# Column sums in column tiles of four, modulation rows moved from pw1 to pw2, and column reductions behind all rows

## The chip, the cores and the metric

The program runs on one core of one Trainium2 chip. The metric is the time that the device takes for one execution, in microseconds (us). Inside a core the engines are named as the profile names them: TensorE (PE for its matmuls, PEld for its weight loads), VectorE (DVE), ScalarE (ACT), GpSimd (POOL) and SyncE (SP), whose queue issues the loads from HBM. Each engine works through its own instructions in the order in which the program holds them; engines wait for each other on semaphores.

## What is computed

The program is a decoder trunk of two layers for one sequence: D = 2048 channels, T = 256 positions, all float32. Layer 0 mixes tokens with a convolution module, layer 1 with attention; a ConvFFN follows each. Only layer 0's mixer and the entry of its FFN bear on the change:

```python
def ada_ln(c, w, b):
    mod = jax.nn.silu(c) @ w + b
    shift, scale, gate = jnp.split(mod, 3, axis=-1)
    return shift[:, None, :], scale[:, None, :], gate[:, None, :]

def conformer_conv_module(h, pw1_w, pw1_b, dw_w, dw_b, ln_g, ln_b, pw2_w, pw2_b):
    u = h @ pw1_w + pw1_b
    val, gt = jnp.split(u, 2, axis=-1)
    u = val * jax.nn.sigmoid(gt)
    u = causal_depthwise_conv(u, dw_w, dw_b)              # width 31
    u = jax.nn.silu(layer_norm(u, ln_g, ln_b))
    return u @ pw2_w + pw2_b
...
    shift, scale, gate = ada_ln(c, mix_mod_w[i], mix_mod_b[i])
    h = rms_norm(x, mix_norm_g[i]) * (1.0 + scale) + shift
    x = x + gate * y                                      # y: the mixer's result for h
    shift, scale, gate = ada_ln(c, ffn_mod_w[i], ffn_mod_b[i])
    h = rms_norm(x, ffn_norm_g[i]) * (1.0 + scale) + shift
    x = x + gate * conv_ffn(h, ...)
```

## The kernel before

**Layout.** Channels lie on the 128 partitions in KD = 16 tiles of 128 channels, positions on the free axis (256 columns). x, the convolution's output ys[0..15] and its products live in SBUF as 128x256 tiles. TensorE's accumulators (PSUM) are eight banks of 512 columns; the names ps, auxa and auxb in the profile are those banks.

**Weights.** Each product streams its weights in "pieces" of eight 128x128 blocks (512 KB, tile `raw`). pw1 multiplies the float32 piece as it is (`pw1_piece`, L612, matmuls at L620). All later products take three passes of a rounded type: `split_next` (L222) makes a high part wh on ScalarE (L230) and a low part wl on VectorE (L234), and `gemm` (L257) issues high x high, high x low and low x high (L283 to L285). SyncE's queue holds all loads in program order (`load`, L211).

**Modulations.** c is one vector, so each modulation vector (2048 values) is a matrix-vector product. The kernel has two ways for it. *Columns*: a tile of 128 outputs by 2048 inputs (1 MB, tile `mraw`) is multiplied and summed on VectorE (`mod_reduce`, L311). *Rows*: a chunk of four 128x512 blocks of the matrix as it lies (1 MB) goes through TensorE (`mod_rows`, L524): four matmuls at L537, each in its own quarter of 32 columns of the array (`tile_position`), add to one bank, auxa; when the rows of a group are complete, ScalarE copies them and TensorE turns them into columns (L552). `load_rows` (L508) loads the chunks ahead; their buffers are a ring of 3 `mraw` and 4 `mrow` tiles (MORE_ROWS). The groups (`rows_of`, L502) are the mixer's gate (16 chunks), the FFN's scale (16 chunks) and the first `rows0` = ROWS = 2 x 512 values of the FFN's shift (8 chunks); the remaining eight tiles of that shift go through VectorE as columns. `mods0` (L566) is the generator of all this: each `advance(fill, 1)` takes one more step. Before pw2 its steps are row chunks; once `nrow["bias"]` is set (L808), two of three steps also issue one column tile (load and reduction).

**The convolution stage** (L697 to L768) is a loop written out by hand: channel tile c = 0 to 16, in each s = 0 to 18. At each s VectorE gets one of the 19 of 31 taps that it computes (`conv_tap`, L643; taps of channels c and c - 1 alternate), ScalarE the products of the other 11 (`conv_prod`, L652), which GpSimd adds up (L737). At s = 0, 7 and 14 TensorE gets pieces of pw1; at the steps of ROWS_AT (L34) a row chunk: one each at s = 11 of c = 1 to 6, 8, 9, 10 and 12, five each in c = 14 and 15, two in c = 16, and ROWS_TAIL = 4 behind the loop. ScalarE's sigmoid and VectorE's product (`gate_act` L625, `gate_mul` L629) make the convolution's input u of channel j from pw1's accumulators.

**The layer norm's sums.** They run over channels, so over partitions: a matmul with `ones_d` (128x128, each 1/2048) adds a tile's partitions into a bank of 256 columns. `y_sum` (L664) does that at s = 3 for channel c - 2: y0 to y7 in one bank, y8 to y15 in another. From the first bank `first_mean` (L670) takes a first mean m1 at c = 11, which is subtracted from every tile (`y_centre`) before it is squared (`y_square`, ScalarE) and its square summed (`y_square_sum`, L683, at the end of each c). Behind the loop dm, var and the reciprocal root follow (L776 to L785), then for each channel z = silu(...) and its two parts (L797, L799, L357, L358), which pw2 multiplies.

**pw2** (L821): 32 pieces; after each, `tick` advances the modulations by RATES["pw2"], 0.65 steps. Its eight first blocks run side by side (`halves=8`). For each finished block, `pw2_done` (L814) scales on ScalarE, adds to x on VectorE (L817) and makes the parts of x for the FFN (`Entry.add`, L418; L424, L425). `need` (L339) drains modulations that are still missing when a consumer asks. Then the FFN's first product (up00a) begins; it needs the reciprocal root of x's mean square (L391) and two columns with the shift (`scaled`, L457, tile bcol).

**Order.** From L722 to the end of the stage, `in_order` (L191) keeps the four compute engines' instructions as the code issues them; elsewhere a scheduler decides, with the gemm's `done` at high priority.

## Time and profile before

| What | us |
|---|---|
| median of 3 runs (2336.69 to 2341.48) | 2337.83 |
| the profiled execution's own time | 2339.05 |
| its span in the profile | 2336.9 |
| TensorE busy (matmuls), in 17812 instructions | 2278.6 (98%) |
| VectorE busy | 1740.2 (74%) |
| ScalarE busy | 1162.2 (50%) |
| GpSimd busy | 263.6 (11%) |

The profile is of one execution; times in it are from the start of its span. In a row of the timeline stand the start, the duration, the engine, the line, the operation, the tiles (written <- read), their shape, how many instructions the row joins, and in brackets how long the engine was idle before it and what ended that. Rows of the chain of waits give start, duration, engine, tile and line of the work that the end of the program hangs on. A row of the windows gives for a stretch its length, the busy time of PE, PEld, DVE, ACT and POOL with the number of instructions, then the granted TensorE clock, the share of the DMA engines and GB/s. A matmul's duration in a row is from its entry to its end; matmuls overlap, so the step from one start to the next is what one costs.

### The profile page before, as it was taken

The page shows a single profiled execution, that of the slowest core. Times are in us where ns is not written, and L with a number is a line of the kernel's source. Part 1 is how long each engine was busy: PE and PEld are TensorE (multiplying, and loading weights), DVE is VectorE, ACT ScalarE, POOL GpSimd, SP SyncE. Part 2 cuts the span into 40 slices and gives each one's busy share as a digit, 9 for nine tenths or more (in the row PEclk, how much of TensorE's full clock was granted, in tenths as well). Part 3 has the DMA queues.
Part 4 walks back from the last instruction along what each step waited for, and adds up shares of the span by engine and source line. Part 5 has one row for each costly group of instructions (what it writes and reads, how often), then busy time and mean ns, then how long its engine had stood idle before and what let it go on. Part 6 is the DMA issues. An engine that isn't in the chain of part 4 may idle for free.

```text
span 2336.9 us, 44053 instructions
## 1 busy us (share of the span) xinstructions
PE 2278.6 (98%) x17812; PEld 2175.1 (93%) x17812; DVE 1740.2 (74%) x2396; ACT 1162.2 (50%) x1766; POOL 263.6 (11%) x339
## 2 busy tenths in 40 slices
PE   7999988999999999999999999999999999999997
PEld 6887667999999999999998999999999999999997
DVE  7689876788888788788876766788887555666654
ACT  2055545755453355554465454657555434555443
POOL 4058602200000000000111110121000000000010
PEclk9999999999999999999999999999999999999999
DMA  9978688577779877778856676775776555555553
GB/s 397 417 302 305 266 345 314 183 280 264 301 275 353 307 284 285 256 280 332 299 187 239 241 245 242 264 283 192 276 275 229 187 189 189 188 187 188 189 190 109
DMA packets 138302, 603.55 MB, mean 258 GB/s; under 512 B 15345, under 2 KB 15473, under 8 KB 113521
## 3 DMA queue, kind: packets, MB, share of 16 engines
q1 hardware_dynamic: 138098, 600.74, 70.8%
q8 instruction: 139, 2.28, 0.4%
q14 instruction: 65, 0.53, 0.1%
HBM read 598.58 MB, written 2.10 MB: 257 GB/s over the span
## 4 chain that ended last, share of the span: by engine, by line
PE 82%; DVE 7%; DMA 6%; issue 3%; ACT 2%; POOL 0%; SPq 0%; DVEq 0%; ACTq 0%; POOLq 0%
PE ps L284 24%; PE ps L283 24%; PE ps L285 24%; PE ps L620 5%; DMA mraw<-in_mt_mix 3%; DVE wl L234 2%; DVE mraw L311 2%; DMA mraw<-in_mt_ffn 1%; PE ps L974 1%; PE ps L975 1%; PE ps L976 1%; PE auxa L537 1%; ACT wh L230 1%; DMA mrow<-in_mr_ffn 1%; DVE hl L358 0%
## 5 line engine op out<-in xcount | busy, mean ns | idle before, releaser
L230 ACT CAST wh<-raw 128x1024 fp32r<-128x1024 f32 x688 | 719.9, 1048 | 770.2 <-PE ps L284 608.5
L234 DVE TENSOR_TENSOR wl<-raw,wh 128x1024 fp32r<-128x1024 f32 x688 | 840.0, 1226 | 350.3 <-ACT wh L230 344.9
L283 PE MATMUL ps<-hh,wh 128*128 128x256 f32 (+1 forms) x3328 | 934.7, 281 | 5.0 <-DVE bcol L460 3.1
L284 PE MATMUL ps<-hl,wh 128*128 128x256 f32 (+1 forms) x3328 | 931.3, 280 | 0.0
L285 PE MATMUL ps<-hh,wl 128*128 128x256 f32 (+1 forms) x3328 | 926.6, 279 | 0.0
L283 PEld LDWEIGHTS ps<-hh,wh 128*128 128x128 f32 x3328 | 625.4, 188 | 6.0 <-issue 3.4
L284 PEld LDWEIGHTS ps<-hl,wh 128*128 128x128 f32 x3328 | 630.4, 189 | 0.2
L285 PEld LDWEIGHTS ps<-hh,wl 128*128 128x128 f32 x3328 | 625.8, 188 | 0.0
L311 DVE CUSTOM_DVE_ANT_0 mraw<-mraw,csr 128x2048 f32<-128x2048 f32 x152 | 349.4, 2299 | 140.4 <-DMA mraw<-in_mt_ffn 72.7
L284 PE MATMUL ps<-gl,wh 128*128 128x256 f32 x1408 | 395.6, 281 | 0.0
L283 PE MATMUL ps<-gh,wh 128*128 128x256 f32 x1408 | 394.5, 280 | 0.1
L285 PE MATMUL ps<-gh,wl 128*128 128x256 f32 x1408 | 393.0, 279 | 0.0
L284 PEld LDWEIGHTS ps<-gl,wh 128*128 128x128 f32 x1408 | 265.8, 189 | 0.0
L283 PEld LDWEIGHTS ps<-gh,wh 128*128 128x128 f32 x1408 | 265.0, 188 | 0.3 <-ACT wh L230 0.3
L285 PEld LDWEIGHTS ps<-gh,wl 128*128 128x128 f32 x1408 | 264.8, 188 | 0.0
L376 POOL TENSOR_TENSOR sumsq<-sumsq,t 128x256 f32<-128x256 f32 x56 | 59.8, 1068 | 1591.6 <-ACT t L372 1591.3
L620 PE MATMUL ps<-hh,raw 128*128 128x256 f32 x832 | 189.9, 381 | 0.0
L620 PEld LDWEIGHTS ps<-hh,raw 128*128 128x128 f32 x832 | 158.1, 191 | 28.7 <-issue 5.0
L839 DVE SCALAR_TENSOR_TENSOR t<-ps,par,t 128x254 f32<-128x254 f32 x336 | 160.8, 479 | 4.1
L643 DVE SCALAR_TENSOR_TENSOR auxb<-u,cpar,auxb 128x256 f32<-128x256 f32 x304 | 125.4, 482 | 4.6 <-ACT auxb L639 3.7
L737 POOL TENSOR_TENSOR y<-y,hl 128x256 f32<-128x256 f32 x144 | 106.3, 739 | 15.9 <-ACT hl L652 5.2
L836 ACT ACTIVATE t<-ps,par 128x256 f32<-128x256 f32 x168 | 94.0, 560 | 2.0 <-PE ps L285 2.0
(175 smaller groups left out, 2099.5 us busy)
## 6 DMA issues: line engine op xcount, KB each, us to landing
raw<-in_w_down SPq DMA_DIRECT2D x176, 512.0 KB, 3.9
mraw<-in_mt_mix SPq DMA_DIRECT2D x80, 1024.0 KB, 7.7
mraw<-in_mt_ffn SPq DMA_DIRECT2D x72, 1024.0 KB, 6.1
raw<-in_w_pw SPq DMA_DIRECT2D x96, 512.0 KB, 8.1
raw<-in_w_up01b SPq DMA_DIRECT2D x84, 512.0 KB, 5.1
raw<-in_w_up11b SPq DMA_DIRECT2D x84, 512.0 KB, 3.5
raw<-in_w_up00b SPq DMA_DIRECT2D x80, 512.0 KB, 5.1
raw<-in_w_up10b SPq DMA_DIRECT2D x80, 512.0 KB, 4.3
```

The source lines that it names most:

```text
L230: nc.scalar.copy(wh[:, :n], v[:, :n])
L234: nc.vector.tensor_tensor(wl[:, :n], v[:, :n], wh[:, :n].bitcast(F32), op=ALU.subtract)
L283: nc.tensor.matmul(o, wh[:, c], xh[kt], start=first, stop=False, skip_group_check=halves > 0)
L284: nc.tensor.matmul(o, wh[:, c], xl[kt], start=False, stop=False, skip_group_check=halves > 0)
L285: nc.tensor.matmul(o, wl[:, c], xh[kt], start=False, stop=left[nb] == 0, skip_group_check=halves > 0)
L311: nc.vector.tensor_tensor_reduce(out=v, in0=v, in1=csr, scale=1.0, scalar=0.0, op0=ALU.mult, op1=ALU.add, accum_out=macc[:, nb:nb + 1])
L376: engine.tensor_tensor(self.sum, self.sum, sq, op=ALU.add)
L620: nc.tensor.matmul(banks[j][:, nb // KD * T:(nb // KD + 1) * T], w[:, b * P:(b + 1) * P], hf[kt], start=first, stop=left[j] == 0, skip_gro ...
L643: nc.vector.scalar_tensor_tensor(conv_ps[j], us[j % UBUFS][:, k:k + T], tap(j, k), conv_ps[j], op0=ALU.mult, op1=ALU.add)
L737: nc.gpsimd.tensor_tensor(ys[c], ys[c], pr, op=ALU.add)
L836: nc.scalar.activation(y, ps[:, :T], AF.Identity, bias=pc(f"fdb{i}", nb, 1), scale=w(FW - 1))
L839: nc.vector.scalar_tensor_tensor(y[:, s:], ps[:, :T - s], w(k), y[:, s:], op0=ALU.mult, op1=ALU.add)
```

## The change

It has four parts.

1. *Column sums.* For the first 14 channels, `col_sum` multiplies with 32 columns of `ones_d` only and places the result in quarter n % 4 of the array, so that four sums go to four groups of 32 rows of one bank. They are issued together, when the fourth channel is there (`y_sums`, at s = 10). `gather` makes one sum of the four groups: ScalarE copies the bank (`gathered`), and a matmul with `ones_q` (each 1/32) adds them up in the bank's upper half. The last two channels are added there as before. The first bank is gathered at s = 3 of c = 10, the second at s = 0 of c = 16, the squares' at s = 4 of c = 16. Square sums are issued at s = 4 of the next channel instead of at the end of the same.
2. *Rows.* ROWS is 3: the FFN's shift goes as rows for 12 of its 16 tiles (44 chunks in all instead of 40) and as columns for four. ROWS_AT puts 23 chunks beside the convolution instead of 22, but only six ahead of c = 13 instead of ten.
3. *Row buffers.* Three more buffers are taken from the weight split tiles (a chunk lies half in a `wh` and half in a `wl`, loaded by two transfers of 512 KB). `row_homes` names each chunk's buffer; the last three ahead of pw2 lie in `mraw`. `load_rows` loads one at a time and is also called once in each of c = 0 to 11.
4. *Column tiles.* In `mods0` the column tiles of the shift come behind all row chunks, no longer between them. And the last split ahead of z (`low`) is issued behind the second z product.

The core of the diff:

```diff
-ROWS = 2
-ROWS_AT = {**{c: (11,) for c in (1, 2, 3, 4, 5, 6, 8, 9, 10, 12)}, 14: (1, 4, 8, 12, 16), 15: (1, 4, 8, 12, 16), 16: (2, 6)}
+SPLIT_ROWS = 3
+ROWS = 3
+ROWS_AT = {**{c: (11,) for c in (2, 4, 6, 8, 10, 12)}, 13: (8, 13, 18), 14: (2, 6, 10, 14, 18), 15: (2, 6, 10, 14, 18), 16: (2, 4, 6, 7)}
...
+    ones_q = const.tile([P, P], F32, name="ones_q")
+    nc.vector.memset(ones_q, 1.0 / 32)
...
+        row_ring = ["m"] * 3 + ["r"] * MORE_ROWS + ["w"] * SPLIT_ROWS
+        row_homes = [row_ring[i % len(row_ring)] for i in range(nrow["near"] - 7)] + ["r"] * 4 + ["m"] * 3
...
-        def load_rows(most=2):
+        def load_rows(most=1):
...
-                more = near and n % (3 + MORE_ROWS) >= 3
-                if len(row_tiles) >= 3 + MORE_ROWS or sum(not t[1] for t in row_tiles) >= (3 if near else 2) and not more:
+                home = row_homes[n] if near else "m"
+                cap = {"m": 3 if near else 2, "r": MORE_ROWS, "w": SPLIT_ROWS}[home]
+                if sum(t[1] == home for t in row_tiles) >= cap:
                     break
...
+                if home == "w":
+                    v = [w_pool.tile([P, PW], F32R, name=x).bitcast(F32) for x in ("wh", "wl")]
+                    for i in range(2):
+                        load(src[:, i * PW:(i + 1) * PW], v[i])
...
         def mods0():
             part = mod_part("ffn0", 0, 4 * cfg.rows0, mark=False) if cfg.rows0 * 4 < KD else iter(())
-            for _ in mod_rows():
-                yield
-                if nrow["bias"]:
-                    nrow["steps"] = nrow.get("steps", 0) + 1
-                    if nrow["steps"] % 3 != 0:
-                        next(part, None)
+            yield from mod_rows()
             yield from part
...
+        def col_sum(ps, n, v, last):
+            g = n % 4
+            nc.tensor.matmul(ps[32 * g:32 * g + 32, :T], ones_d[:, 0:32], v, start=n < 4, stop=last,
+                             tile_position=(0, 32 * g))
+
+        def gathered(ps):
+            v = t256()
+            nc.scalar.copy(v, ps[:, :T])
+            return v
+
         def y_sum(j):
-            b = j >= M0
-            if j in (0, M0):
-                st[b] = psum_acc()
-            nc.tensor.matmul(st[b][:, :T], ones_d, ys[j], start=j in (0, M0), stop=j in (M0 - 1, KD - 1))
...
+            if j < KD - 2:
+                n, ps, end = (j, st["y0"], M0) if j < M0 else (j - M0, st["y1"], KD - 2 - M0)
+                col_sum(ps, n, ys[j], n + 4 >= end)
+            else:
+                nc.tensor.matmul(st["y1"][:, T:2 * T], ones_d, ys[j], start=False, stop=j == KD - 1,
+                                 skip_group_check=True)
+
+        def y_sums(j):
+            waiting.append(j)
+            if j in (3, 7, 11) or j >= KD - 3:
+                while waiting:
+                    y_sum(waiting.pop(0))
+
+        def gather(name):
+            v = gathered(st[name])
+            nc.tensor.matmul(st[name][:, T:2 * T], ones_q, v, start=True, stop=name == "y0", skip_group_check=True)
...
         def y_square_sum(j, sq):
-            nc.tensor.matmul(st["sq"][:, :T], ones_d, sq, start=j == 0, stop=j == KD - 1)
+            n = nsq["n"]
+            nsq["n"] += 1
+            if n < KD - 2:
+                col_sum(st["sq"], n, sq, n >= KD - 6)
+            else:
+                nc.tensor.matmul(st["sq"][:, T:2 * T], ones_d, sq, start=False, stop=n == KD - 1,
+                                 skip_group_check=True)
...
+            if c < M0 + 4:
+                load_rows()
...
+                if s == 4:
+                    for j, sq in squared:
+                        y_square_sum(j, sq)
+                    squared = []
+                    if c == KD:
+                        gather("sq")
+                if s == 3 and c == M0 + 2:
+                    gather("y0")
...
-                    y_sum(c - 2)
+                    if c == KD:
+                        gather("y1")
+                        y_sum(c - 2)
+                if s == 10 and 1 < c < KD:
+                    y_sums(c - 2)
...
-            for j, sq in squared:
-                y_square_sum(j, sq)
...
-        low()
-        nc.vector.tensor_tensor(dm, dm, st[1][:, :T], op=ALU.add)
+        nc.vector.tensor_tensor(dm, dm, st["y1"][:, T:2 * T], op=ALU.add)
...
+            if j == 1:
+                low()
```

More of the change, by code (lines that the diff above doesn't have):

```diff
@@ L537, in mod_rows @@
                             nc.tensor.matmul(ps[32 * g:32 * g + 32, :], hot[:, k0 + g, 31 - i:63 - i],
-                                             v[:, g * 512:(g + 1) * 512], start=first, stop=last,
+                                             v[g], start=first, stop=last,
                                              tile_position=(0, 32 * g))
@@ L662, in hybrid_trunk @@
         JC = M0 + 2
[L664 to L668 removed]
+        def col_sum(ps, n, v, last):
[6 more added lines that the diff above has]
+            return v
+        def y_sum(j):
+            if j == 0:
+                st["y0"] = psum_acc()
+            if j == M0:
+                st["y1"] = psum_acc()
+            if j < KD - 2:
[12 more added lines that the diff above has]
+            nc.tensor.matmul(st[name][:, T:2 * T], ones_q, v, start=True, stop=name == "y0", skip_group_check=True)
         def first_mean():
[L671 to L672 removed]
+            nc.scalar.activation(m1, st["y0"][:, T:2 * T], AF.Copy, scale=KD / M0)
+            nc.vector.scalar_tensor_tensor(dm, m1, (KD - JC) / KD - 1.0, st["y0"][:, T:2 * T], op0=ALU.mult, op1=ALU.add)
             st["sq"] = psum_acc()
@@ L788, in hybrid_trunk @@
             advance(fill, 1)
-        assert not any(more for _, more in row_tiles)
+        assert all(home == "m" for _, home in row_tiles)
         early.close()
```

17 lines of the change are left out of this document (10 added, 7 removed).

## The prediction

> **What bounds the kernel now.** I read first the chain of waits on the page, then the windows of 100 us, to see where a shorter step would reach the end of the program at all.
>
> ```profile
> PE 82%; DVE 7%; DMA 6%; issue 3%; ACT 2%; POOL 0%; SPq 0%; DVEq 0%; ACTq 0%; POOLq 0%
> ...
> 500.00:600.00 100.00, 100.00 (x860) 100.00 (x859) 82.36 (x105) 50.64 (x70) 0.00 (x0) 1.00 0.75 282
> ```
>
> The chain is TensorE for 82%, and from 500 us on its windows are full (100.00 of 100.00), so what is gained earlier arrives at the end unchanged, and nothing behind 500 us is touched. The change lies between 137 and 430 us: the convolution with pw1 beside it, then pw2. The chain of waits within the first part (start, duration, what):
>
> ```profile
> 164.95 1.00 PE auxa L537 x8
> 165.95 3.65 PE ps L620 x16
> 169.60 0.43 PE ps L668 x2
> ...
> 173.48 0.99 PE auxa L537 x8
> ...
> 265.81 3.45 PE ps L620 x16
> 269.26 0.45 PE ps L684 x2
> ...
> 270.14 3.99 ACT hl L652 x10
> 274.13 0.37 ACT t L625
> 274.53 0.50 DVE u L629
> ...
> 281.06 0.99 PE ps L552 x8
> ```
>
> One channel tile c costs TensorE 173.48 - 164.95 = 8.53 us: two pieces of pw1 of 3.45 (as at 265.81), a row chunk (L537) of 0.99, a column sum (L668) of 0.43, and 0.20 more for the piece behind a row (3.65 against 3.45). A row beside pw1 therefore costs 1.19 us, a sum 0.43. But VectorE keeps the same pace; its timeline, with ScalarE's and TensorE's around the first mean:
>
> ```profile
> 220.14 0.48 DVE L629 SCALAR_TENSOR_TENSOR u<-ps,cpar,t 128x256 f32<-128x256 f32 x1 [0.82 <-ACT t L625]
> 227.59 2.45 DVE L643 SCALAR_TENSOR_TENSOR auxb<-u,cpar,auxb 128x256 f32<-128x256 f32 x6 [0.24 <-ACT auxb L639]
> 232.46 0.42 DVE L672 SCALAR_TENSOR_TENSOR dm<-m,ps 128x256 f32<-128x256 f32 x1 [2.42 <-ACT m L671]
> ...
> 274.53 0.48 DVE L629 SCALAR_TENSOR_TENSOR u<-ps,cpar,t 128x256 f32<-128x256 f32 x1 [4.58 <-ACT t L625]
> ```
>
> ```profile
> 220.00 4.08 ACT L652 ACTIVATE hl<-u,cpar 128x256 f32<-128x256 f32 x10
> ...
> 232.05 0.38 ACT L671 ACTIVATE m<-ps 128x256 f32<-128x256 f32 x1 [3.66 <-PE ps L668]
> ```
>
> ```profile
> 231.42 0.59 PE L668 MATMUL ps<-y,ones_d 128*128 128x256 f32 x2
> ```
>
> VectorE waits for TensorE's work only three times: 0.82, 2.42 (first mean, for the sum of y7 at 231.42) and 4.58 us, the last because ScalarE stood until L684 gave a buffer back at 269.7. Those 7.8 us are all that a faster TensorE can give in this stage, whatever it saves itself.
>
> Then pw2. First the row chunk between two pieces, the number of its matmuls, and what holds it:
>
> ```profile
> 301.13 0.70 PE L283 MATMUL ps<-zh,wh 128*128 128x256 f32 x4 [0.66 <-ACT zh L357]
> ...
> 301.90 0.28 PE L283 MATMUL ps<-zh,wh 128*128 128x256 f32 x1
> ...
> 303.91 0.28 PE L285 MATMUL ps<-zh,wl 128*128 128x256 f32 x1
> 304.12 1.07 PE L537 MATMUL auxa<-mraw,hot 128*32 128x512 f32 x8
> 305.11 0.75 PE L283 MATMUL ps<-zh,wh 128*128 128x256 f32 x4
> ...
> 330.38 0.74 PE L283 MATMUL ps<-zh,wh 128*128 128x256 f32 x4 [2.26 <-ACT zh L357]
> ```
>
> ```profile
> L285 PE MATMUL ps<-zh,wl x256: 275/279/416, 301.8 to 429.5; 128*128 128x256 f32 x128
> ```
>
> From 301.90 to 303.91 lie 17 steps: 0.118 us for a matmul, 90.8 us for 768. The group at 304.12 sets the next matmul back by 1.08 us and the one behind by another 0.12: 1.2 us for each visit of row matmuls. pw2 takes 301.1 to 429.5 = 128.4 us; with 15 visits (18.0) and two turns of rows into columns (L552) of 0.99, 110.8 are work, and **17.6 us are lost**. Where:
>
> ```profile
> 318.55 2.28 DVE L311 CUSTOM_DVE_ANT_0 mraw<-mraw,csr 128x2048 f32<-128x2048 f32 x1
> ...
> 389.69 2.29 DVE L311 CUSTOM_DVE_ANT_0 mraw<-mraw,csr 128x2048 f32<-128x2048 f32 x1 [2.09 <-DMA mraw<-in_mt_ffn]
> ```
>
> ```profile
> 320.81 0.33 SPq L212 DMA_DIRECT2D mraw<-in_mr_ffn  x1
> ...
> 322.19 1.19 SPq L212 DMA_DIRECT2D raw<-in_w_pw  x2
> ```
>
> ```profile
> 328.49 1.04 ACT L230 CAST wh<-raw 128x1024 fp32r<-128x1024 f32 x1 [4.57 <-DMA raw<-in_w_pw]
> ```
>
> ```profile
> 366.00:368.00 2.00, 0.30 (x5) 0.10 (x1) 1.17 (x3) 2.00 (x5) 0.73 (x1) 1.00 0.95 381
> ...
> 370.00:372.00 2.00, 2.00 (x13) 2.00 (x12) 2.00 (x3) 1.34 (x3) 1.02 (x1) 0.55 0.99 408
> ```
>
> Eight reductions (L311, 2.28 us; the first and the last are shown) stand in VectorE's order between the splits. SyncE's queue waits for them too: at 320.81 it goes on when the reduction of 318.55 has given its buffer back, so weights issued at 322.19 reach ScalarE 4.57 us late, which waits in order ahead of zh, and TensorE stops 2.26 us at 330.38. The granted clock falls to 0.55 (third figure from the end of the row) at 370 behind a pause (0.30 us busy in 366 to 368): 13 matmuls in those 2 us where 17 fit.
>
> **The change part by part.** Columns in fours. The trace has no such sum of 256 columns, but row groups do the like with 512:
>
> ```profile
> 272.11 2.78 PE L537 MATMUL auxa<-mrow,hot 128*32 128x512 f32 x24
> ```
>
> Three chunks of four column tiles in 2.78 us, 0.87 each in a run: two passes of 0.43 in which four run side by side, as 512 columns alone would take. A group of four sums should thus cost 0.43 to 0.6 us; one after another would be 4 x 0.43 = 1.72. I take 0.6, by the row with the same form.
>
> Up to the last piece TensorE loses four rows (4.8), twelve sums (5.2) and two square sums (0.9), and gets four groups (2.4) and a gather (0.43): 8.1 us earlier, so that 269.3 becomes 261.2. What of it arrives? The sum of y4 to y7 now stands at s = 10 of c = 9, a piece behind the old y7, and ScalarE has to copy it in its order at s = 3 of c = 10. Before, ScalarE ahead of the first mean (u_252 is channel 10, hl its products for GpSimd, auxb the first tap of channel 11, m the mean):
>
> ```order
> L652 ACTIVATE hl_1662<-u_252,cpar 128x256
> L652 ACTIVATE hl_1666<-u_252,cpar 128x256
> L652 ACTIVATE hl_1670<-u_252,cpar 128x256
> L652 ACTIVATE hl_1685<-u_252,cpar 128x256
> L652 ACTIVATE hl_1689<-u_252,cpar 128x256
> L652 ACTIVATE hl_1693<-u_252,cpar 128x256
> L639 ACTIVATE auxb<-u_253,cpar 128x256
> L652 ACTIVATE hl_1705<-u_252,cpar 128x256
> L652 ACTIVATE hl_1709<-u_252,cpar 128x256
> L671 ACTIVATE m_269<-ps 128x256
> ```
>
> and now (u_254 is channel 10):
>
> ```order
> L661 ACTIVATE hl_1644<-u_254,cpar 128x256
> L682 COPY t<-ps 128x256
> L661 ACTIVATE hl_1653<-u_254,cpar 128x256
> L661 ACTIVATE hl_1657<-u_254,cpar 128x256
> L661 ACTIVATE hl_1661<-u_254,cpar 128x256
> L661 ACTIVATE hl_1676<-u_254,cpar 128x256
> L661 ACTIVATE hl_1680<-u_254,cpar 128x256
> L661 ACTIVATE hl_1684<-u_254,cpar 128x256
> L648 ACTIVATE auxb<-u_255,cpar 128x256
> L661 ACTIVATE hl_1696<-u_254,cpar 128x256
> L661 ACTIVATE hl_1700<-u_254,cpar 128x256
> L710 ACTIVATE m_271<-ps 128x256
> ```
>
> The copy (L682) is new; it stands behind three products of channel 10 and ahead of six and of auxb. ScalarE comes to it at 220.0 + 4 x 0.41 = 221.6. TensorE ends the group at 231.4 - 3.6 (three rows) - 3.0 (seven sums) + 0.6 (first group) + 3.65 (the piece) + 0.6 = 229.7. So ScalarE stands 8 us; then copy 0.4, six products 2.5, auxb 0.4 like a product: 233.0. Behind auxb wait VectorE's taps from s = 12 on (the 0.24 at 227.59 is this wait), six taps in 2.45, and the first mean comes at 235.5 instead of 232.46, **3.0 us later**. Yet the third wait goes: the square sums now stand at s = 4, the last piece is 8 us earlier, and VectorE reaches u of channel 15 at 269.95 (274.53 - 4.58) + 3.0 = 273.0 instead of 274.53. Gain so far 1.5 us.
>
> At the end of the stage:
>
> ```profile
> 287.84 0.70 PE L668 MATMUL ps<-y,ones_d 128*128 128x256 f32 x2 [1.60 <-DVE y L676]
> ...
> 292.90 0.70 PE L668 MATMUL ps<-y,ones_d 128*128 128x256 f32 x2 [0.90 <-DVE y L676]
> ```
>
> ```profile
> 293.90 0.41 DVE L779 TENSOR_TENSOR dm<-dm,ps 128x256 f32<-128x256 f32 x1
> ```
>
> ```profile
> 300.58 0.40 ACT L357 CAST zh<-t 128x256 fp32r<-128x256 f32 x1 [1.33 <-PE auxa L537]
> ```
>
> y14's sum starts 1.5 earlier, 286.3; in TensorE's order four rows (3.6), a group (0.6) and the gather of the squares with ScalarE's copy (1.2) now stand between it and y15's: 0.6 + 5.4 brings 292.3 instead of 292.90, though VectorE would be ready at 291.4. Of 1.5 us 0.6 is left. The split ahead of L779 is moved behind two products of z, where VectorE waits for zh. Last, zh waited 1.33 us for the last row in a buffer of the closed pool; now the three last rows stand in mraw and only one of the other kind is in the tail: -1.3. **Convolution: -2 us**, at one end +1 (groups one after another hold the copy 2.6 longer), at the other -6 (the copy holds nobody, and most of the 7.8 goes).
>
> The ten buffers: rows in wh and wl are two transfers of 512 KB; those tiles are free until pw2's first split, behind the last piece of pw1; their last row is read at c = 16, s = 2, so I cost this at nothing; if the split had to wait for that row, about 1 us. The other two copies stand where ScalarE waits for y14 anyway. The fill of ones_q lies in the opening, which waits for DMA.
>
> **pw2.** 17 row chunks instead of 14, and by the order in 20 visits instead of 15 (three chunks are parted 1 + 3): +6.0 us of work. The eight reductions leave; four come back at the very end, four are rows now. With them go the stops of SyncE behind their buffers. What is left to lose are the z chain of the first tiles and the draining of eight sums, and I take that 6 of the 17.6 us stay, since the stop at 330.38 follows a weight that waited for a reduction, and the slow clock a pause: -11.6 + 6.0, about **-6 us** (2 lost: -10; 14 lost: +2). The end of pw2 on VectorE, before (x the residual, hl its low half, wl a split):
>
> ```order
> L234 TENSOR_TENSOR wl<-raw,wh 128x1024 x2
> L817 TENSOR_TENSOR x<-x,t 128x256
> L425 SCALAR_TENSOR_TENSOR hl_3602<-x,a_ffn_2853,hh_3601 128x256
> L234 TENSOR_TENSOR wl<-raw,wh 128x1024 x2
> L817 TENSOR_TENSOR x<-x,t 128x256
> L425 SCALAR_TENSOR_TENSOR hl_3674<-x,a_ffn_2853,hh_3673 128x256
> L234 TENSOR_TENSOR wl<-raw,wh 128x1024 x2
> L391 RECIPROCAL rstd<-t 128x256
> ```
>
> and now:
>
> ```order
> L314 ISA mraw,macc<-mraw,csr 128x2048
> L314 ISA macc 128x1
> L877 TENSOR_TENSOR x<-x,t 128x256
> L237 TENSOR_TENSOR wl<-raw,wh 128x1024
> L314 ISA mraw,macc<-mraw,csr 128x2048
> L314 ISA macc 128x1
> L428 SCALAR_TENSOR_TENSOR hl_3668<-x,a_ffn_2808,hh_3667 128x256
> L237 TENSOR_TENSOR wl<-raw,wh 128x1024
> L314 ISA mraw,macc<-mraw,csr 128x2048
> L314 ISA macc 128x1
> L394 RECIPROCAL rstd<-t 128x256
> ```
>
> Of the four reductions (ISA mraw; the first, a tile earlier, isn't shown) two now stand ahead of the last x and two between it and the reciprocal, with the splits parted between them.
>
> ```profile
> 437.76 1.75 DVE L391 RECIPROCAL rstd<-t 128x256 f32<-128x256 f32 x1
> ```
>
> ```profile
> 455.76 0.36 PE L283 MATMUL ps<-hh,wh 128*128 128x256 f32 x1 [1.69 <-DVE bcol L460]
> ```
>
> From pw2's end (429.5) to the reciprocal lay 8.3 us; two reductions behind x and part of one ahead of it, 4.6 to 6.8 us, come into them, and VectorE's waits there for the last block's way through ScalarE take some of it up. I put the reciprocal 3 later; behind it stand the modulated tiles, and TensorE waits for VectorE there already (1.69). I take +1.5 us (0 to 4; the 4 if the last column tile, whose buffer the first reduction frees, lands late and holds SyncE's weights behind it).
>
> Sum against the profiled execution (2339.05, span 2336.9): -2 - 6 + 1.5 = -6.5. That execution is 1.2 above the median of 2337.83, which I shift: 2331.3.
>
> In the sum the half clock of 370 goes with the pause of 366, which holds at most 1.70 us. [...]
>
> **The rivals.** *Visits add, waits stay* (0.12): TensorE's 17.6 us in pw2 may belong to the chain mul, silu, zh, zl and to the draining, which the change leaves; then +6 for visits, with -2 and +1.5: +5.5, **2343.3**, slower. It decides once more than 17 us stay lost. For it: the wait of 0.66 for zh at 301.13 has no reduction near. Against: the stop at 330.38 has its late weight in the trace.
>
> *Reductions at a bad place* (0.20): the four at the end, 9.1 us, delay splits and reciprocal by all that VectorE's waits don't take up; up00 gets +5 instead of +1.5: -3, **2334.8**, no change.
>
> *Half clock in the convolution* (0.08): TensorE, faster now, has nothing between its rows of c = 14 (about 271.5) and the squares of c = 15 (275.6); after such a gap the clock may fall as at 370, and a run of four rows ahead of y15 that meets it takes up to 3.6 more, 2.5 as a middle: -4, **2333.8**. The pause is longer than that of 366, which speaks for it. [...]
>
> *The copy holds nobody* (0.12): if TensorE's group is there before ScalarE, the convolution gives -6: -10.5, **2327.3**. Against: 8 us of distance.
>
> That four sums do not run side by side is in the convolution's upper end.
>
> **How the numbers follow.** The forecast has 0.48. A measurement of this kernel tells about 0.2%, 4.7 us, from no change (below 2333.1, above 2342.5). Faster: 0.46 of the forecast and the 0.12 of the last rival, 0.58; same: 0.02 + 0.20 + 0.08 = 0.30; slower 0.12. The range 2325 to 2339 leaves out the slower rival and some of the far gains.
>
> **What would show it.** In the changed profile: groups L676 of about 0.5 us; ScalarE's L682 with a wait of some 8 us near 222 and VectorE's with 5 to 6 behind auxb; no wait of 4.6 at channel 15; pw2's first matmul near 299; between it and the first hh matmul about 122 us with 20 visits; no wait for weights of 4 us; the reciprocal some 11 us behind pw2's end. It is wrong if pw2 takes over 126 us, if the pause of ScalarE is missing, or if up00 loses over 4 us.

## The result, and the profile after

The changed kernel takes 2328.3 us in the median of six runs (2325.1 to 2332.8), the kernel before 2341.1 in six runs beside it (2336.7 to 2346.3): a ratio of 0.9939, interval 0.9924 to 0.9954. It is faster by about 12.8 us, twice the 6.5 forecast, and inside the range. The profiled execution, the fastest of the six, took 2325.1 us; its span is 2322.9, 14.0 less than that of before. TensorE's share of the chain that ended last rises from 82% to 87%, and DMA's falls from 6% to 4%, by the page:

```profile
PE 87%; DVE 7%; DMA 4%; ACT 1%; issue 1%; POOL 0%; SPq 0%; DVEq 0%; ACTq 0%; POOLq 0%
```

Where the 14 us arose is read from the first matmul of each product, as a view of one tile's instructions gives it. The rows name the line, the number of matmuls, the shortest, median and longest duration in ns, and the start of the first and the last one. After:

```profile
L286 PE MATMUL ps<-zh,wh x256: 274/280/388, 300.0 to 415.8; 128*128 128x256 f32 x128
...
L286 PE MATMUL ps<-hh,wh x3328: 274/280/468, 416.1 to 2185.2; 128*128 128x256 f32 x184, 128*128 128x258 f32 x12
...
L286 PE MATMUL ps<-gh,wh x1408: 274/280/286, 681.3 to 2309.2; 128*128 128x256 f32 x176
```

Before, the rows of x's parts (hh) and of the FFN's second product (gh, the gated tiles):

```profile
L283 PE MATMUL ps<-hh,wh x3328: 274/280/468, 429.6 to 2199.3; 128*128 128x256 f32 x184, 128*128 128x258 f32 x12
...
L283 PE MATMUL ps<-gh,wh x1408: 274/280/357, 692.1 to 2323.3; 128*128 128x256 f32 x176
```

| stage | before | after | difference | forecast |
|---|---|---|---|---|
| start to the first matmul with z | 301.1 | 300.0 | -1.1 | -2 |
| pw2, to the first matmul with x's parts (hh) | 128.5 | 116.1 | -12.4 | -6 |
| the FFN's first product, to the first with gh | 262.5 | 265.2 | +2.7 | +1.5 |
| the rest, to the end of the span | 1644.8 | 1641.6 | -3.2 | 0 |

The change ends with the third row: -10.8. The last row is not put to it: that stretch takes 1641.0 to 1649.2 us in the profiles of the runs below, though no kernel changes anything there. One part of the attention alone, from the first to the last matmul of the product at L974 of the kernel before (1199.8 to 1431.7, 231.9 us), took 229.2 us in the profile of a_mix and 238.2 in that of a_conv.

**The convolution** went as the prediction's steps said up to 273 us. ScalarE, VectorE and TensorE around the first gather:

```profile
229.69 0.37 ACT L682 COPY t<-ps 128x256 f32<-128x256 f32 x1 [9.70 <-PE ps L676]
```

```profile
232.95 2.45 DVE L652 SCALAR_TENSOR_TENSOR auxb<-u,cpar,auxb 128x256 f32<-128x256 f32 x6 [6.94 <-ACT auxb L648]
...
294.35 0.42 DVE L837 TENSOR_TENSOR dm<-dm,ps 128x256 f32<-128x256 f32 x1 [3.21 <-PE ps L694]
```

```profile
228.90 0.64 PE L676 MATMUL ps<-y,ones_d 128*32 128x256 f32 x8
...
274.80 1.24 PE L676 MATMUL ps<-t,ones_d 128*32 128x256 f32 x4 [4.38 <-ACT t L719]
...
287.63 0.59 PE L694 MATMUL ps<-y,ones_d 128*128 128x256 f32 x2
...
293.54 0.70 PE L694 MATMUL ps<-y,ones_d 128*128 128x256 f32 x2
...
300.03 0.71 PE L286 MATMUL ps<-zh,wh 128*128 128x256 f32 x4 [1.35 <-ACT zh L360]
```

The copy came at 229.69 (forecast 229.7) with a wait of 9.70 us (8), VectorE stood 6.94 us behind it (5 to 6), the first mean came at 235.30 (235.5), and the wait of 4.58 at channel 15 is gone. Four sums side by side are real: eight matmuls, which are two passes of four, in 0.57 us to the next start (228.90 to 229.47). From there on the stage ran late: y14's sum (the row of 287.63) was expected at 286.3. What stands there is a pause of 4.38 us on TensorE ahead of the square sums of c = 15, and the granted clock behind it (third figure from the end of a window's row; before, these windows have 1.00 throughout):

```profile
272.00:274.00 2.00, 0.00 (x0) 0.00 (x0) 2.00 (x6) 0.16 (x1) 1.76 (x4) 0.91 1.02 408
274.00:276.00 2.00, 1.20 (x9) 0.95 (x13) 1.76 (x5) 2.00 (x6) 0.44 (x1) 0.50 1.08 440
...
284.00:286.00 2.00, 2.00 (x14) 0.40 (x6) 1.93 (x6) 0.10 (x1) 0.64 (x1) 0.50 1.02 430
286.00:288.00 2.00, 2.00 (x10) 0.82 (x4) 1.90 (x5) 0.00 (x0) 0.00 (x0) 0.68 0.99 418
288.00:290.00 2.00, 2.00 (x21) 0.65 (x22) 1.86 (x5) 0.00 (x0) 0.00 (x0) 1.00 1.03 434
```

That is the rival *half clock in the convolution*, which had a chance of 0.08: 0.50 from about 273.6 to 287.3. The first row of 272 holds 0.91, so 0.36 us of it were slow; the row of 286 holds 0.68, so 1.28 us. TensorE works through rows and sums there at half speed (the eight row matmuls at 278.87 take 1.94 us; the eight at 299.41 of the kernel before, at a clock of 1.00, 1.07), and VectorE then waits 3.21 us for the sum of y15.

**pw2** has no stop left. Its two halves, before and after:

```profile
300.00:350.00 50.00, 46.24 (x362) 37.75 (x358) 38.71 (x66) 24.04 (x40) 0.00 (x0) 1.00 0.86 334
350.00:400.00 50.00, 41.79 (x294) 32.34 (x287) 32.75 (x49) 26.00 (x53) 11.86 (x9) 0.93 0.85 327
```

```profile
300.00:350.00 50.00, 49.97 (x381) 40.01 (x384) 35.20 (x65) 30.43 (x50) 0.00 (x0) 1.00 0.87 335
350.00:400.00 50.00, 50.00 (x406) 41.44 (x400) 29.65 (x38) 29.16 (x50) 10.57 (x12) 1.00 0.82 316
```

TensorE is busy for 99.97 of 100 us instead of 88.03, at full clock. With 90.8 us for the matmuls with z and 2.0 for the turns, 116.1 leaves 23.3 for 20 visits: 1.165 each (the prediction had 1.2). This price takes it that the changed kernel lost nothing, and its trace bears that out: between the first matmul with z and the first with hh TensorE's idle times add up to 0.0 us. By this price the kernel before lost 128.5 - 92.8 - 15 x 1.165 = 18.2 us; its trace has 11.3 us of idle time there and 6.8 us at a clock of 0.50, which cost 3.4; the other 3.5 us were not parted further.

**The FFN's first product** starts with the reductions on VectorE:

```profile
417.44 2.28 DVE L314 CUSTOM_DVE_ANT_0 mraw<-mraw,csr 128x2048 f32<-128x2048 f32 x1
...
424.87 2.28 DVE L314 CUSTOM_DVE_ANT_0 mraw<-mraw,csr 128x2048 f32<-128x2048 f32 x1
...
427.08 1.74 DVE L394 RECIPROCAL rstd<-t 128x256 f32<-128x256 f32 x1
```

```profile
440.14 0.39 PE L288 MATMUL ps<-hh,wl 128*128 128x258 f32 x1 [2.47 <-DVE wl L237]
```

The reciprocal stands 11.0 us behind pw2's end (8.3 before), as forecast. But the next stop is not the one at bcol: TensorE waits 2.47 us for a split, which VectorE reaches late. Behind this wait the granted clock is 0.50 from 440.9 to 444.3, which costs another 1.7 us.

### The profile page after: what moved, and what is told of

Its sections match the earlier page's. It is cut to its first block, busy times and chain, and to the rows that moved or that the text cites. A ratio compares the mean times of both kernels' runs of the same rounds, so it can differ in the third digit from the quotient of the medians.

```text
span 2322.9 us, 44140 instructions
## 1 busy us (share of the span) xinstructions
PE 2277.3 (98%) x17850; PEld 2170.8 (93%) x17850; DVE 1732.6 (75%) x2389; ACT 1164.3 (50%) x1769; POOL 263.2 (11%) x339
## 4 chain that ended last, share of the span: by engine, by line
PE 87%; DVE 7%; DMA 4%; ACT 1%; issue 1%; POOL 0%; SPq 0%; DVEq 0%; ACTq 0%; POOLq 0%
PE ps L286 25%; PE ps L287 25%; PE ps L288 25%; PE ps L629 4%; DMA mraw<-in_mt_mix 3%; DVE mraw L314 2%; PE auxa L551 2%; DVE wl L237 1%; PE ps L1034 1%; PE ps L1035 1%; PE ps L1036 1%; DVE auxb L652 1%; DMA mraw<-in_mt_ffn 1%; DVE hl L361 0%; DVE rstd L394 0%
## 5 line engine op out<-in xcount | busy, mean ns | idle before, releaser
L288 PE MATMUL ps<-hh,wl 128*128 128x256 f32 (+1 forms) x3328 | 927.6, 279 | 2.5 <-DVE wl L237 2.5
L288 PEld LDWEIGHTS ps<-hh,wl 128*128 128x128 f32 x3328 | 626.7, 188 | 2.8 <-DVE wl L237 2.7
L314 DVE CUSTOM_DVE_ANT_0 mraw<-mraw,csr 128x2048 f32<-128x2048 f32 x148 | 339.4, 2293 | 118.0 <-DMA mraw<-in_mt_mix 59.8
L288 PE MATMUL ps<-gh,wl 128*128 128x256 f32 x1408 | 393.1, 279 | 0.0
L288 PEld LDWEIGHTS ps<-gh,wl 128*128 128x128 f32 x1408 | 264.9, 188 | 0.0
L786 POOL TENSOR_TENSOR y<-y,hl 128x256 f32<-128x256 f32 x144 | 106.8, 742 | 23.3 <-ACT hl L661 12.5
```

The lines of the kernel that those rows point to most:

```text
L288: nc.tensor.matmul(o, wl[:, c], xh[kt], start=False, stop=left[nb] == 0, skip_group_check=halves > 0)
L314: nc.vector.tensor_tensor_reduce(out=v, in0=v, in1=csr, scale=1.0, scalar=0.0, op0=ALU.mult, op1=ALU.add, accum_out=macc[:, nb:nb + 1])
L786: nc.gpsimd.tensor_tensor(ys[c], ys[c], pr, op=ALU.add)
```

## The experiments

Times below are medians; a ratio is to the kernel before, measured beside it, with its 95% interval. "z" is the start of the first matmul with z, "pw2" the time from there to the first matmul with hh, "FFN" from there to the first with gh. "Lost" is pw2 less 92.8 and 1.165 for each visit of row matmuls, the visits counted in the order of instructions.

| run | us | ratio | z | pw2 | visits | lost | FFN |
|---|---|---|---|---|---|---|---|
| before | 2341.1 | 1 | 301.1 | 128.5 | 15 | 18.2 | 262.5 |
| changed | 2328.3 | 0.9939 (0.9924 to 0.9954) | 300.0 | 116.1 | 20 | 0.0 | 265.2 |
| a_mix | 2326.4 | 0.9931 (0.9910 to 0.9952) | 299.0 | 118.9 | 18 | 5.1 | 262.5 |
| a_red | 2331.0 | 0.9952 (0.9937 to 0.9968) | 298.8 | 121.2 | 20 | 5.1 | 265.4 |
| a_dma | 2332.0 | 0.9955 (0.9938 to 0.9972) | 298.7 | 121.1 | 18 | 7.3 | 267.9 |
| b_pw2 | 2333.0 | 0.9951 (0.9930 to 0.9972) | 299.8 | 117.8 | 21 | 0.5 | 266.4 |
| a_conv | 2339.7 | 0.9990 (0.9976 to 1.0003) | 298.8 | 124.0 | 14 | 14.9 | 265.4 |
| i_late | 2328.2 | 0.9942 (0.9927 to 0.9957) | 300.2 | 121.3 | 20 | 5.2 | 262.7 |
| a_red8 | 2333.7 | 0.9964 (0.9951 to 0.9977) | 298.9 | 123.9 | 21 | 6.6 | 264.8 |
| a_warm | 2325.1 | 0.9928 (0.9908 to 0.9948) | 301.3 | 116.1 | 20 | 0.0 | 265.2 |
| i_gather | 2323.8 | 0.9927 (0.9910 to 0.9944) | 296.1 | 116.2 | 20 | 0.1 | 265.2 |
| i_tail | 2325.2 | 0.9929 (0.9914 to 0.9944) | 297.8 | 118.0 | 21 | 0.7 | 264.9 |
| i_gather2 | 2323.3 | 0.9925 (0.9909 to 0.9941) | 298.0 | 117.7 | 20 | 1.6 | 266.0 |
| i_fill | 2321.5 | 0.9913 (0.9898 to 0.9927) | 296.1 | 116.2 | 20 | 0.1 | 265.2 |

The theory at the start: the eight reductions in VectorE's order, and SyncE's stops behind their buffers, made the whole loss of pw2. The rivals: the bytes of the column tiles made it, or the chain of z did.

**a_mix: the four column tiles back among the rows.**

```diff
-            yield from mod_rows()
+            for _ in mod_rows():
+                yield
+                if nrow["bias"]:
+                    nrow["steps"] = nrow.get("steps", 0) + 1
+                    if nrow["steps"] % 3 != 0:
+                        next(part, None)
             yield from part
```

> The changed kernel, with its four remaining column tiles put back among the row chunks of pw2 (two of three steps, as before the change). pw2 is counted from its first matmul with z to the first matmul of the next product: 128.5 us before the change (301.1 to 429.6), 116.1 after it (300.0 to 416.1). Theory A, the reductions in VectorE's order and SyncE's stops behind their buffers made the lost time: half of the reductions are back, so 4 to 9 us of the 17.6 are lost again, pw2 120 to 125, and the end of pw2 wins about 2.7 because VectorE is free there; the whole 2 to 6 us slower than the changed kernel. Theory B, it was the bytes (eight tiles of 1 MB in pw2): about the same, 4 MB more at some 0.4 MB per us, up to 10 us. Theory C, the lost time belonged to the chain of z and the draining, and something else in the change took it: pw2 stays at 116 to 117. This run tells C from A and B.

pw2 lost 5.1 us, of which two visits fewer give 2.3 back, and the FFN's start won 2.7. From z to gh that is 381.4 us, against 381.3 in the changed kernel. So reductions among the rows do cost, theory C falls, and *to put the column tiles behind all rows is worth nothing by itself*: what pw2 wins, the FFN's start pays. The expected 2 to 6 us slower did not come.

**a_red: VectorE's time without the bytes**, and **a_dma: the bytes and their buffers without VectorE's time.** Results of the added work are thrown away.

```diff
# a_red, at the steps of a_mix; nrow["old"] is a tile of 128x2048 in SBUF
+    nc.vector.tensor_tensor_reduce(out=nrow["old"], in0=nrow["old"], in1=csr, scale=1.0, scalar=0.0,
+                                   op0=ALU.mult, op1=ALU.add, accum_out=held.pop())
+    held.append(cpool.tile([P, 1], F32, name=f"scr{n}"))
+    load(io["mt_ffn0"][n % 4, :, 0:1], held[0])
# a_dma
+    nc.vector.tensor_copy(scr[:, len(have) % 4:len(have) % 4 + 1], held.pop()[:, 0:1])
+    held.append(mod_load("ffn0", 4 * cfg.rows0 + n % 4))
```

> The changed kernel, with four more reductions of 128x2048 on VectorE among the row chunks, of a tile in SBUF that nothing loads; each waits only for a load of one number per partition, at the place where the column tile's load stood. The results are thrown away. So VectorE's time is there, but neither the bytes nor a buffer for which SyncE must wait. Theory A1, VectorE's 2.3 us in front of the splits and of z's low parts is enough: pw2 119 to 123 instead of 116.1. Theory A2, it takes SyncE's stop behind the buffer: pw2 116 to 117. Theory B, bytes: 116 to 117.

> The changed kernel, with four more loads of column tiles (1 MB each) among the row chunks; their buffer is given back by a copy of one column on VectorE, without a reduction; the column tiles at the end of pw2 stay too. So the bytes and the buffer are there, but not the 2.3 us on VectorE. Theory A1, VectorE's time: pw2 116 to 117.5. Theory A2 (buffers) or B (bytes): 119 to 126, with waits of ScalarE's or VectorE's splits for weights.

Each by itself costs pw2 time: 5.1 us lost with VectorE's time, 7.3 with the loads. So A1 holds, and so does A2 or B. a_dma doesn't part these two, since its loads bring the bytes as well as a buffer for which SyncE's queue must wait. Together, in a_mix, they lose no more than VectorE's time does. The place differs. In a_red TensorE waits while z is still being made:

```profile
312.11 0.39 PE L286 MATMUL ps<-zh,wh 128*128 128x256 f32 x1 [1.17 <-ACT wh L233]
...
331.15 0.74 PE L286 MATMUL ps<-zh,wh 128*128 128x256 f32 x4 [0.83 <-ACT zh L360]
```

In a_dma it waits while the first eight sums are drained, for splits that are late. At 344.54 the view names the copy that gives the column tile's buffer back (scr), but that copy stands behind the split wl of 343.26, which the matmul reads, and VectorE had waited 1.91 us for the wh ahead of that split:

```profile
344.54 0.39 PE L288 MATMUL ps<-zh,wl 128*128 128x256 f32 x1 [0.76 <-DVE scr L590]
...
350.15 0.39 PE L288 MATMUL ps<-zh,wl 128*128 128x256 f32 x1 [0.39 <-DVE wl L237]
...
362.01 0.39 PE L288 MATMUL ps<-zh,wl 128*128 128x256 f32 x1 [0.76 <-DVE wl L237]
```

**a_red8: eight reductions without bytes.** The edit is that of a_red with twice as many steps.

```diff
-                    if n in (1, 2, 4, 5, 7):
+                    if n in (1, 2, 4, 5, 7, 8, 10, 11, 13):
```

> As the run a_red (more reductions among the row chunks of pw2, of a tile that nothing loads, results thrown away), with eight instead of four, as many as before the change. Four cost pw2 5.1 us there, without bytes and without a buffer that SyncE waits for; the eight of the kernel before went with 17.6, of which the change won 12.4 and the convolution part alone 4. Theory A, VectorE's time alone, linear: 10 us, pw2 126 to 127. Theory B, several reductions push each other's weights late and the slow clock follows: 14 to 18, pw2 130 to 134. Theory C, four more reductions cost little without the bytes of the tiles: pw2 121 to 123.

pw2 123.9: the second four cost 1.5 us more (6.6 lost against 5.1). Theory A, a linear price, is out, and so is B; C is nearest. The loss of 18.2 us before the change therefore takes more than VectorE's time. Eight loads without reductions were not run.

**b_pw2: the pw2 part alone**, on the kernel before.

```diff
-ROWS = 2
+ROWS = 3
...
-            for _ in mod_rows():
...
+            yield from mod_rows()
             yield from part
```

> The kernel before, with only the third group of rows (ROWS = 3) and the column tiles behind all rows: the pw2 part of the change without its convolution part. 18 chunks are left for pw2. If the parts add up: the convolution ends as before (first matmul with z at 301 us), pw2 takes 116.1 + 1.2 = 117 to 118, the next product loses 2.7, the whole about 8 us faster than before. Rival, pw2 is fast only because the convolution part leaves it a better start (more buffers, last rows in other buffers): pw2 over 121, the whole 4 us faster or less.

pw2 117.8, 0.9951: the pw2 part has most of the gain (11.5 us by this ratio, where 8 were expected), and no better start from the convolution is needed.

**a_conv: the convolution part alone** (ROWS = 2 and the interleaving of a_mix, in the changed kernel).

> The changed kernel with ROWS = 2 and with the column tiles among the row chunks again: the convolution part of the change (sums in fours, fewer rows beside pw1, ten row buffers) without its pw2 part. If the parts add up: first matmul with z at 299 to 300 (before 301.1), pw2 with 13 chunks and eight reductions 126 to 128, so that the whole is 1 to 4 us faster than before, a tenth to a quarter of what the change gives. Rival: the four reductions of the run a_mix cost pw2 only 2.8 us where the eight of the kernel before went with 17.6, so the new row buffers may have helped: then pw2 is 119 to 122 here too, and the whole 7 to 10 us faster.

z at 298.8 and a whole of 0.9990 (0.9976 to 1.0003): 2.3 us, not told from none. pw2 lost 14.9 with eight reductions and 13 chunks, a little less than before; the 124.0 lie between the expected 126 to 128 and the rival's 119 to 122, so neither came. a_conv and a_mix differ in ROWS alone, eight column tiles among the rows against four and four row chunks more: from z to gh they take 389.4 and 381.4 us, and the whole 2339.7 and 2326.4. Eight tiles with their bytes cost three times what four cost, and the second half of pw2 shows how:

```profile
362.92 0.39 PE L286 MATMUL ps<-zh,wh 128*128 128x256 f32 x1 [2.79 <-ACT t L881]
```

```profile
360.00:365.00 5.00, 2.21 (x16) 2.08 (x13) 3.26 (x6) 3.79 (x9) 2.18 (x3) 0.87 0.98 403
365.00:370.00 5.00, 5.00 (x37) 5.00 (x36) 4.49 (x6) 3.15 (x5) 2.06 (x2) 0.79 0.73 303
...
390.00:395.00 5.00, 4.21 (x21) 3.92 (x22) 3.90 (x16) 4.59 (x13) 0.00 (x0) 0.60 0.78 288
395.00:400.00 5.00, 5.00 (x34) 5.00 (x33) 2.90 (x3) 1.12 (x2) 0.00 (x0) 0.71 0.79 265
```

A stop of 2.79 us, behind the reduction that VectorE began at 356.02 in the midst of draining the eight sums, and then the granted clock below 1: the slow stretches begin at 363.7 and 391.0, each less than 1 us behind a stop (2.79 and 1.87 us). Of the 14.9 us TensorE was idle for 8.4, and 10.2 us at a clock of 0.50 cost 5.1; the four tiles of a_mix bring stops of at most 0.82 and no slow clock in pw2.

**i_late: column tiles only from the tenth step on**, where VectorE is half idle.

```diff
-                    if nrow["steps"] % 3 != 0:
+                    if nrow["steps"] > 9:
```

> The changed kernel, with its four column tiles one by one behind the 10th to 13th step of pw2's rows, neither from the start (a_mix) nor behind all rows. Theory A: reductions cost pw2 something only while z and its parts are still being made (to 345 us) and while the first eight sums are drained; later VectorE is busy for half of its time, so pw2 stays at 116 to 117.5 and the next product wins the 2.7 us that the four reductions cost at its start (first matmul of the second FFN product 2.5 us earlier than in the changed kernel, at 677.5 to 679.5). Rival B, any reduction among the splits costs 0.7 us: pw2 118.9, like a_mix, and the whole is the same as the changed kernel.

Theory A fell: pw2 121.3, 5.2 us lost (rival B had 2.8), and 2.5 won at the FFN's start; the whole is the changed kernel's. One late weight made most of the loss, with 3.4 us of slow clock behind it, which cost 1.7:

```profile
391.27 0.38 PE L286 MATMUL ps<-zh,wh 128*128 128x256 f32 x1 [2.02 <-ACT wh L233]
392.53 0.39 PE L288 MATMUL ps<-zh,wl 128*128 128x256 f32 x1 [0.76 <-DVE wl L237]
```

```profile
390.00:395.00 5.00, 2.97 (x16) 2.77 (x17) 4.31 (x5) 1.30 (x3) 0.72 (x1) 0.81 1.02 415
395.00:400.00 5.00, 5.00 (x36) 4.03 (x36) 2.80 (x6) 2.29 (x6) 0.00 (x0) 0.84 1.01 408
```

SyncE's queue at that time:

```profile
379.25 0.42 SPq L215 DMA_DIRECT2D raw<-in_w_pw  x1
380.02 0.33 SPq L215 DMA_DIRECT2D mraw<-in_mt_ffn  x1
386.00 0.33 SPq L215 DMA_DIRECT2D mraw<-in_mr_ffn  x1
386.38 1.62 SPq L215 DMA_DIRECT2D raw<-in_w_pw  x2
```

For six us it issued no weights: next in it stood a row chunk, into the mraw buffers that the column tiles use too, and the weights behind it. It went on when the reduction of 383.68 had ended. An idle VectorE is not enough; the queue's order counts.

**i_gather: the copy earlier.** Sum of y4 to y7 at s = 6, gather ahead of the piece.

```diff
+                if s == 0 and c == M0 + 2:
+                    gather("y0")
                 if s in (0, 7, 14)[:upto[c] - (upto[c - 1] if c else 0)]:
                     pw1_piece(next(pw1))
...
-                if s == 3 and c == M0 + 2:
-                    gather("y0")
...
-                if s == 10 and 1 < c < KD:
+                if s == (6 if c < M0 + 2 else 10) and 1 < c < KD:
```

> The changed kernel, with the sum of y4 to y7 a piece earlier (s = 6 instead of 10) and its gather at s = 0 of c = 10, ahead of the piece, instead of s = 3. Theory A (the copy stops ScalarE, which stops VectorE's taps, which set the pace): the copy of the first bank comes at 226 instead of 229.7 and its wait falls from 9.7 to about 5 us, VectorE's from 6.9 to about 4; the first mean is 2.9 earlier, TensorE's pause of 4.4 at 270 gets shorter, and the first matmul with z comes at 296 to 297.5 instead of 298.7 to 300.0. Rival: the end of the convolution hangs on TensorE's rows and sums of c = 15 and 16; then nothing arrives.

```profile
226.41 0.37 ACT L682 COPY t<-ps 128x256 f32<-128x256 f32 x1 [7.04 <-PE ps L676]
```

```profile
230.47 2.44 DVE L652 SCALAR_TENSOR_TENSOR auxb<-u,cpar,auxb 128x256 f32<-128x256 f32 x6 [4.27 <-ACT auxb L648]
```

```profile
283.63 0.70 PE L694 MATMUL ps<-y,ones_d 128*128 128x256 f32 x2 [2.04 <-DVE y L715]
...
296.13 0.71 PE L286 MATMUL ps<-zh,wh 128*128 128x256 f32 x4 [1.07 <-ACT zh L360]
```

As theory A says: VectorE's wait fell by 2.7 us and z came 2.6 to 2.9 earlier than in the five kernels with the same convolution that began at 298.7 to 299.0. The slow clock doesn't make this difference: in those five y14's sum stands behind a wait of 2.0 us for VectorE, at 286.2 to 286.5, so the slow stretch ahead of it was taken up there, and here it stands behind the same wait at 283.63. ScalarE's wait at the copy is what set the pace. With 0.9927 this is a version faster than the kernel before and, in its median, 4.5 us faster than the changed one, though the two intervals overlap.

**i_gather2: the copy behind ScalarE's products.**

```diff
-                if s == 3 and c == M0 + 2:
+                if s == 12 and c == M0 + 2:
                     gather("y0")
-                if s in (0, 7, 14)[...]:
+                if s in ((12, 13, 14) if c == M0 + 2 else (0, 7, 14))[...]:
```

> The changed kernel with the sum of y4 to y7 at s = 6 of c = 9 (as in the run i_gather), its gather at s = 12 of c = 10, behind ScalarE's products and the first tap of channel 11, and the two pieces of pw1 of c = 10 behind the gather (s = 12 and 13 instead of 0 and 7). Theory A (ScalarE's stop at the copy is what holds VectorE): the copy still comes at 226 to 226.5, now with a wait of less than 3 us; VectorE's wait behind the first tap of channel 11 (6.9 us in the changed kernel, 4.3 in i_gather) goes; the first mean is taken at 228.5 to 230 instead of 235.4; the first matmul with z comes at 293 to 295.5, and the whole is 4 to 6 us faster than the changed kernel. Rival B, TensorE waits for the copy and its pieces come later: the last piece of pw1 ends at 263 instead of 261.5 and TensorE's rows at c = 15 and 16 hold the sums; first matmul with z no earlier than in i_gather (296).

```profile
226.51 2.45 DVE L652 SCALAR_TENSOR_TENSOR auxb<-u,cpar,auxb 128x256 f32<-128x256 f32 x6 [0.25 <-ACT auxb L648]
```

```profile
231.62 0.38 ACT L710 ACTIVATE m<-ps 128x256 f32<-128x256 f32 x1 [4.05 <-PE ps L707]
```

VectorE's wait behind the tap is gone (0.25 us), but the first mean came at 232.0, not 229: the gather's matmul stood behind a piece of pw1 and a row chunk, and ScalarE waited 4.05 us for it. y14's sum began at 282.81, 0.8 us earlier than in i_gather. z came at 298.0, a miss: the clock was 0.50 from 282.1 to 289.0, and from y14's sum to y15's TensorE took 8.7 us, where it took 6.0 in i_gather. A second slow stretch, 299.2 to 302.6, made the 1.6 us lost in pw2.

**i_tail: two rows behind y15's sum; a_warm and i_fill: TensorE's pauses filled.** In a_warm and i_fill the added matmuls go to the free half of a bank in whose other half sums of the layer norm are being added up. The output of i_fill is not the program's; of both only the time is used.

```diff
# i_tail, on i_gather
-... 16: (2, 4, 6, 7)}
-ROWS_TAIL = 4
+... 16: (2, 4)}
+ROWS_TAIL = 6
# a_warm, on the changed kernel, at s == 4 of c == KD - 1; i_fill, on i_gather: 3 there and 4 ahead of y14's sum, in st["sq"]
+                        for _ in range(10):
+                            nc.tensor.matmul(st["y1"][:, T:2 * T], ones_d, ys[0], start=True, stop=True,
+                                             skip_group_check=True)
```

> As i_gather, and the last two rows of c = 16 (s = 6 and 7) moved behind the sum of y15 (ROWS_TAIL 6 instead of 4). Theory: y15's sum waits for these two rows, 1.7 us, though y15 is ready (VectorE waited 3.2 us for it), and behind the sum TensorE has 5 us with nothing but four rows while the root and the first z are made: 1 to 2 us earlier than i_gather. Rival: the rows in buffers of the closed pool then end later and hold the first z: same time or later than i_gather.

> The changed kernel with ten more matmuls of 128x256 in TensorE's pause ahead of the square sums of c = 15 (their result goes to half a bank that is not used yet and is overwritten). The pause of 4.4 us at 270 is filled, the work behind it is the same. Theory A, the slow clock at 275 to 287 (mean 0.66 in 270 to 290) comes from the pause and costs the end of the convolution: the granted clock stays 1.0, the sum of y14 comes at 286 to 286.7 instead of 287.6, TensorE's rows ahead of y15's sum end earlier too, and the first matmul with z comes 1 to 2 us earlier, at 298 to 299. Rival, the clock falls all the same or y15's sum hangs on VectorE and ScalarE alone: no change.

> The run i_gather (sum of y4 to y7 a piece earlier, gather ahead of the piece) with TensorE's two longest pauses in the end of the convolution filled: three more matmuls of 128x256 ahead of the square sums of c = 15, where it waited 1.7 us, and four ahead of the sum of y14, where it waited 2.0 us; their results go to half a bank that is not used yet. In the profiles so far the granted clock was 0.5 for 3 to 13 us somewhere between 273 and 290 in every kernel with the new convolution, except i_gather's, which has a first matmul with z at 296.1; where the slow stretch lay on the sums of y14 and y15 (i_tail, a_warm, i_gather2) the wait for y15's sum was 0.6 to 2.7 us longer. Theory A, the pauses bring the slow clock: it stays 1.0 from 262 to 295, first matmul with z at 296 to 297, the median at or below i_gather's 2323.8. Rival B, the slow clock comes whatever stands in the pauses: a stretch at 0.5 shows up, and z begins at 297 to 299.

In a_warm the clock stays at 1.00 where it was 0.50, and falls behind the next pause instead:

```profile
286.10 1.22 PE L694 MATMUL ps<-y,ones_d 128*128 128x256 f32 x2 [2.04 <-DVE y L715]
```

```profile
276.00:278.00 2.00, 0.85 (x7) 0.00 (x0) 1.97 (x6) 2.00 (x6) 1.65 (x3) 1.00 1.04 426
...
284.00:286.00 2.00, 0.06 (x1) 0.00 (x0) 1.93 (x6) 0.00 (x0) 0.59 (x1) 0.79 1.03 430
286.00:288.00 2.00, 1.90 (x6) 0.70 (x10) 1.89 (x5) 0.00 (x0) 0.00 (x0) 0.50 1.01 422
288.00:290.00 2.00, 2.00 (x16) 0.58 (x11) 1.86 (x5) 0.00 (x0) 0.00 (x0) 0.50 1.01 418
290.00:292.00 2.00, 1.74 (x14) 0.21 (x4) 0.96 (x3) 0.13 (x1) 0.00 (x0) 0.51 0.99 412
```

y14's sum came at 286.10, as theory A says. But there the slow clock (285.2 to 292.0) lies on the way from y14's sum to y15's, and z comes at 301.3, later than without the filling. i_tail has the same code as i_gather up to that place and the same pause of 2.03 us, but the slow clock (282.8 to 289.6), and z at 297.8; so it cannot say what its own edit does, and theory and rival stay open there. In i_fill the longest pause is 1.39 us and the clock is 1.00 throughout, but i_gather's profile has 1.00 as well: both begin z at 296.1. Its median is 2.3 us below i_gather's, with intervals that overlap. That the pause brings the slow clock is shown by a_warm, where it moved, beside the seven profiles in which the pause was left and the clock fell in it each time. What filling saves on average is not shown.

## Why the prediction was right, and where it was off

The direction, the range and the path were right; the forecast size was half of what was measured, mostly by one term. In the pair of profiles (14.0 us against 6.5) pw2 gives 6.4 of the 7.5 us between them, the convolution and the FFN's start take 2.1 back, and 3.2 stand in the rest, which no term explains.

- *Convolution, -2.* The pause at the copy, the price of a group, the vanished third wait and, in the profiles where the slow clock was short, the gain at the tail were as worked out. The stage's gain is -1.1 in the profile of the change and -2.1 to -2.4 in five others with the same convolution, which differ by the slow clock: 13.6 us of it in the one (and in i_late, where z came at 300.2), 3.4 in a_mix and a_conv. b_pw2, with the convolution of before, had z at 299.8 instead of 301.1, so that 1.3 us of these differences may be what this stage varies by, and single profiles don't tell the part's gain closer than 0 to 2.4 us. The rival *half clock in the convolution* thus came true beside the forecast, at 1.0 to 1.3 us, less than the 2.5 us put on it.
- *pw2, -6.* The mis-sized term is "I take that 6 of the 17.6 us stay". Nothing stayed (0.0, and 0.5 in b_pw2). The 6 us were given to the chain of z and to the draining of eight sums; in the changed kernel that chain runs beside the matmuls, with a first wait of 1.35 us and none behind it. The rival *visits add, waits stay* fell with it: the visits did add, 5 x 1.165 = 5.8 us, but the waits were not the chain's.
- *Why the waits go.* The prediction gave it to the reductions leaving pw2. The runs part this further: four reductions fewer, by four more row chunks, carry the gain (8.0 us from z to gh between a_conv and a_mix); that the other four stand behind all rows moves it from pw2 to the FFN and is worth 0.1 us (a_mix).
- *FFN's start, +1.5.* +2.7, inside the 0 to 4. a_mix and i_late, without the four reductions there, have 262.5 and 262.7, so the 2.7 come with the reductions. But only 0.9 of it is more waiting (3.6 us of idle time against 2.7); 1.7 is the stretch of slow clock behind the late split (mean 0.83 from 440 to 450), which the sum did not have. a_conv, also without reductions there, has 265.4: its page counts 1.8 us in which TensorE, at the products with hh, waits for late splits (L288), and none of it lies ahead of 460.
- *The rest, 0.* -3.2 in the pair of profiles, but this stretch varies by more between the profiles of the runs, so it is not put to the change. What varies there stays open; slow clock in the attention doesn't make the -3.2, for each profile of the pair has 3.4 us of it behind 1220 (mean 0.83 from 1235 to 1245 before, 0.66 from 1225 to 1230 after).

Open: why eight column tiles lose 15 to 18 us where four lose 5 and eight reductions without bytes 6.6. That late weights, stops of about 2 us and more and the slow clock come together there is seen, and the stops come first. Whether the bytes or the wait for a buffer make the weights late was not tried.

## What to carry to other kernels

A step that is moved behind a stage pays at the head of the next one (here 2.7 us, by a_mix): cost both ends before calling a stage won. When one transfer queue serves weights and other tiles, look at who shares its buffers, not only at which engine is idle: in i_late the queue issued no weights for six us. And where an engine works in order, place a copy that waits for another engine behind the work that others wait for, or give what it waits for sooner. Here a sum and its copy moved one piece earlier brought about 2.7 us (i_gather); the copy behind ScalarE's products took VectorE's wait away (i_gather2), but z came no earlier in its one profile.
